# Expert stage of a three-block kernel: token parts moved from GpSimd to VectorE, and a new pinned order of an expert's steps

## The chip, the cores and the metric

The kernel runs on one core of one Trainium2 chip. The time is the device time of one execution in microseconds (us). 512 tokens pass through two dense blocks and then through a block that ends in a mixture of 32 experts.

## The reference, cut to what matters

The dense blocks (attention, convolution, a state-space mixer) are untouched by the change. What the change touches is the last part, for 512 tokens of 1024 features:

```python
combine = jnp.sum(jax.nn.one_hot(expert_id, N_EXPERTS, dtype=f32) * w[..., None], axis=1)
y = jnp.zeros_like(xt)
for e in range(N_EXPERTS):                      # 32
    h = jax.nn.silu(xt @ w_gate[e]) * (xt @ w_up[e])      # 1024 -> 256, twice
    y = y + combine[:, e:e + 1] * (h @ w_down[e])         # 256 -> 1024
```

Each token has two experts; their weights and places follow from a router that runs just before.

## The kernel before, in words

**Tiling.** The router sorts the 1024 pairs of token and expert by expert (`route`, L1536). The rows of the tokens are fetched in sorted order by indirect DMAs, transposed on TensorE, and kept in one tile `XT`, with features down the partitions and sorted places along the columns. Expert i takes 96 columns of `XT` from a place that is known only at run time (128 for one further job, number 32, that takes the overflow of a large expert). A loop over still more overflow closes the stage; its bound is read at run time.

**Two-part values.** A float32 product is made of three TensorE passes. Each operand is split into a high part (rounded to fp32r) and a low part (the value less its high part), and `mm3` (L298 to L300) multiplies high by high, high by low and low by high. So every weight tile needs a copy on ScalarE (`mh`, step h, L1716) and a subtraction on VectorE (`ml`, step l, L1722); each expert has six such pairs of 128x1024, numbered 0 to 5: 0 to 3 are gate and up weights, 4 and 5 are down weights. The expert's token columns need the same (`xh` and `xl`, step x, `tokens`, L1762).

**The steps of an expert** (`Expert.step`, L1710). x: token parts. h, l: weight parts. g0 to g3: six passes each of 128x512 into a PSUM tile `acc`. s: SiLU on ScalarE (L1734). m: product on VectorE (L1736), and the row numbers `ix` (L1738). t: two transposes on TensorE (L1742). a, b: parts of the transposed tile (ScalarE L1745, VectorE L1747). d0, d1: six passes each into a PSUM tile `s`. y0, y1: copies of the two halves into a tile `ye` on ScalarE (L1757); after y1 GpSimd issues an indirect DMA (L1759) that adds the 96 rows of `ye` to the output in DRAM.

**Order.** `moe` (L1432) walks over the 33 jobs. In one round, x is the round's expert, `prev` the one before, and `nxt` the one after. The string `MOE` (L67) is the order in which the steps are traced: h, l, g and the small x belong to the round's expert, H, L and X to the next one, the other letters to the one before. From round 2 on (`CHAIN`), `in_order` (L1489) makes every engine and the queues of SyncE and GpSimd take their instructions exactly in the traced order; before that the scheduler decides.

**Buffers and queues.** The raw weights come in three DMAs of 1 MB per expert, issued by SyncE, into a ring of nine tiles, so the next load into a tile waits for both subtractions that read it. `mh` has seven tiles, `ml` six, `ye` three, `xh` and `xl` two. The adds of rows into the output all write the same DRAM tensor, and each waits until the one before has landed. The first nine raw tiles are loaded during the block before.

**GpSimd's work before.** From expert 2 on (`POOL = 2`) `tokens` reads the place into a GpSimd register (L1769), makes `xh` with a copy (L1775) and `xl` with a subtraction (L1776), both on GpSimd. For experts 0 and 1 ScalarE and VectorE do it (L1771, L1772). The first four subtractions of expert 0 (`LPOOL = 4`) also run on GpSimd, ahead of the router; all other subtractions of experts 0 and 1 are held until the router's sort is done (`issue_after`).

Of the kernel before, what the change touches and what calls it, by code (L numbers as in the profile page):

```python
# [9 lines left out]
F32 = mybir.dt.float32  # L10
# [4 lines left out]
AF = mybir.ActivationFunctionType  # L15
OP = mybir.AluOpType
AX = mybir.AxisListType
PSUM = bass.MemoryType.PSUM
# [41 lines left out]
NRAW = (6, 2, 0, 1)  # L60
POOL = 2
LPOOL = 4
AHEAD = 2
CHAIN = 2
EXTRA = 29
ORDERED = (mybir.EngineType.PE, mybir.EngineType.Activation, mybir.EngineType.DVE, mybir.EngineType.Pool, mybir.EngineType.SP)
MOE = "X s m h2 g0 t a l2 b h3 g1 h4 d0 y0 l3 l4 h5 l5 d1 y1 H0 L0 g2 H1 L1 g3"  # L67
RW1 = (0, 0, 0, 0, 0, 0, 0, 0)
# [166 lines left out]
def prior(offset):  # L235
    """A method whose instructions the scheduler takes earlier, by so many places."""
    def deco(f):
        def g(self, *a, **k):
            with self.tc.high_priority(offset=offset):
                return f(self, *a, **k)  # L240
        return g
    return deco


class K:
# [36 lines left out]

# [1 line left out]
    def psum(self, pool, tag, shape=(128, 512)):  # L284
# [105 lines left out]
    def positions(self, pf):  # L390
        """Positions as float32, along the row and (negated) down the partitions."""
        nc, A = self.nc, self.A
        pi = self.T(self.xp, [128, 512], F32, "sq").bitcast(I32)
        nc.gpsimd.dma_start(pi, A["pos"].to_broadcast([128, 512]))
        nc.vector.tensor_copy(pf, pi)
        qi = self.T(self.smp, [128, 8], I32, "nyi")[:, :4]
        nc.gpsimd.dma_start(qi, A["pos"].rearrange("a (t p) -> p (a t)", p=128))
        posq = self.T(self.smp, [128, 4], F32, "posq")
        nc.vector.tensor_copy(posq, qi)
        nc.vector.tensor_scalar(posq, posq, -1.0, None, op0=OP.mult)  # L400
        return posq
# [14 lines left out]
    def distances(self, pf, posq):  # L416
        """Position biases of all heads, to DRAM."""
        nc = self.nc
        dist = self.T(self.ap, [128, QW], F32, "E")
        for t in range(4):  # L420
            n = 128 * (t + 1)
            nc.scalar.activation(dist[:, QOFF[t]:QOFF[t] + n], pf[:, :n], AF.Abs, bias=posq[:, t:t + 1])
        for h in range(6):
            B = self.T(self.ap, [128, QW], F32, "E")
            nc.vector.tensor_scalar(B, dist, -(2.0 ** (-8.0 * (h + 1) / 6)) * 32.0 ** 0.5, None, op0=OP.mult)
            nc.gpsimd.dma_start(self.Bd[h], B)
# [11 lines left out]

# [1 line left out]
    def x_in(self):  # L440
# [39 lines left out]

# [1 line left out]
    @prior(200)  # L482
    def pv(self, E, vt, hd, u):
        """E: probabilities up to a factor per query [128, QW]; writes the head's rows (head hd of a pair) of u."""
        nc = self.nc
# [28 lines left out]
    def vtile(self, src, part=None):  # L514
        """src: a pair's feature-major values, or a tile per head with its rows in part; gives token-major two-part tiles."""
        nc = self.nc
        vt = self.T(self.ap, [128, 2, 4, 2, 64], F32R, "V")
        bank = self.psum(self.pt, "t")
        bv = bank.rearrange("p (k b c) -> p k b c", k=4, b=2)
        ident = self.c("ident")  # L520
        for k in range(4):
            c = slice(128 * k, 128 * k + 128)
            if part is None:
                nc.tensor.transpose(bank[:, c], src[:, c], ident)
            else:
                for b in range(2):
                    nc.tensor.transpose(bv[:, k, b, :], src[b][part, c], ident[part, part])
        d = vt.rearrange("p b k a c -> p k b a c")
        self.split(d[:, :, :, 0, :], d[:, :, :, 1, :], bv)
        return vt  # L530

    @prior(200)
    def softmax(self, score, sm, bias=None, scale=1.0, mask=None):
        """Rows of one score map: exp(logit - max) in a [128, QW] tile, their sums per query tile in sm [128, 4]."""
        nc = self.nc
# [25 lines left out]
    def bcast2(self, f):  # L561
        """f: a factor per token and head of a pair [128, 4, 2]; gives it for the pair's feature rows (PSUM)."""
        pt = self.psum(self.pt, "t")
# [11 lines left out]
    def square_sums(self, u, r=None):  # L575
        """Per token and head of a pair: the sum of squares of u, times r twice."""
        nc = self.nc
# [9 lines left out]

# [1 line left out]
    def layer(self, l):  # L589
# [13 lines left out]
    def attention(self, l):  # L603
# [47 lines left out]
        def spill(i):  # L651
            """M-tile i of the projection, as exact two-part values, to DRAM."""
            acc = mtile(i)
# [25 lines left out]
        def norm_out(us, rs, sq, name):  # L679
            """Norm over all pairs; sq: their square sums per token and head."""  # L680
            v = sq[0]
# [270 lines left out]

# [1 line left out]
    def mixer(self):  # L954
# [28 lines left out]
        def gate(i, spare, d=None):  # L983
            """sigmoid of gate tile i; kept on chip, or in DRAM."""
            acc = mtile(i, spare)
# [111 lines left out]
    def moe_in(self):  # L1097
        """What the experts need that does not depend on their tokens."""
        nc, A, M = self.nc, self.A, self.rt
# [29 lines left out]
    def x_out(self, x, m, gain, racc):  # L1129
        """A finished tile of the residual stream: to the output and, times the gain, to the rows the experts read."""  # L1130
        nc = self.nc
# [20 lines left out]
    def sin_cos(self, pool, ang, k, lo, shape, sin_scale):  # L1152
        """ang: exact multiples (reduced in place by k turns), lo: what is added after; gives (cos, sin * sin_scale)."""
        nc = self.nc
# [213 lines left out]
    def forget_spill(self, mtile, R, p, j):  # L1368
        """Queries (j = 0) or keys (1) of a pair, normalised, as two-part values, or its values (2): to DRAM."""
        nc, sp = self.nc, self.sp  # L1370
# [55 lines left out]

# [1 line left out]
    def mc(self, name):  # L1428
# [3 lines left out]
    def moe(self):  # L1432
        nc, tc, A = self.nc, self.tc, self.A
        with ExitStack() as c:
# [31 lines left out]
            x = start(0)  # L1466
            x.run("x h0 l0 h1 l1")
            for n in range(len(seq)):
# [3 lines left out]
                for what in MOE.split():  # L1472
                    k, j = what[0], int(what[1:] or 0)
                    if k in "hlgx":
                        y = x
# [6 lines left out]
                prev, x = x, nxt  # L1482
            prev.run("s m t a b d0 y0 d1 y1")
            self.in_order(mark)
# [4 lines left out]
    def in_order(self, mark):  # L1489
        """Each engine takes what was traced since mark in the order in which it was traced."""  # L1490
        last = {}
# [6 lines left out]
    def dynamic(self, i):  # L1498
        """The i-th of the jobs on the list: its weights, records, what drops its empty rows, and its place."""
        nc = self.nc  # L1500
# [9 lines left out]
    def records(self, off, n):  # L1510
        """Token, weight and norm factor of n sorted places from off."""
        nc = self.nc
# [8 lines left out]
    def first_max(self, x, m, n, iota):  # L1521
        """One-hot of the first maximum along the last axis of x [128, m, n], and the maximum."""
        nc, P = self.nc, self.rt
# [172 lines left out]
class Expert:  # L1696
    """One run of rows through one expert's weights, in steps."""

    def __init__(self, K, i, we, sl, big, off, n=128):
        """off: where the first of the n columns of XT stands, on chip (None: at 0)."""  # L1700
        self.K, self.i, self.sl, self.big, self.off, self.n = K, i, sl, big, off, n
# [8 lines left out]
    def step(self, k, j):  # L1710
# [6 lines left out]
        elif k == "l":  # L1717
            hi, lo, w = self.W[j]
            pool = (self.i, j) < (0, LPOOL)
            after = K.tc.issue_after(K.routed) if self.i < 2 and not pool else ExitStack()  # L1720
            with after:
                (nc.gpsimd if pool else nc.vector).tensor_tensor(lo, w, hi.bitcast(F32), op=OP.subtract)  # L1722
        elif k == "x":
# [38 lines left out]
    def tokens(self):  # L1762
        K, n, nc = self.K, self.n, self.K.nc
        self.x = x = tuple(K.T(K.mx, [128, KD, n], F32R, t) for t in ("xh", "xl"))

        def cols(eng):
            if self.off is None:
                return K.XT[:, :, 0:n]
            return K.XT[:, :, bass.ds(eng.value_load(self.off, min_val=0, max_val=2 * S), n)]  # L1769
        if self.i < POOL:  # L1770
            nc.scalar.activation(x[0], cols(nc.scalar), AF.Copy)  # L1771
            nc.vector.tensor_tensor(x[1], cols(nc.vector), x[0].bitcast(F32), op=OP.subtract)  # L1772
        else:
            src = cols(nc.gpsimd)
            nc.gpsimd.tensor_copy(x[0], src)  # L1775
            nc.gpsimd.tensor_tensor(x[1], src, x[0].bitcast(F32), op=OP.subtract)  # L1776

# [16 lines left out]
```

## Time and profile before

| what | value |
|---|---|
| median of 3 runs | 2154.57 us |
| lowest and highest run | 2150.1 and 2155.29 us |
| span of the profiled execution | 2153.1 us (its whole time was not recorded apart from the span) |
| TensorE busy | 94% of the span |
| VectorE busy | 71% |
| ScalarE busy | 51% |
| GpSimd busy | 10%, nearly all of it in the last sixth |

The span is divided by the page into 40 slices. In the last eight, the expert stage with the router ahead of it, VectorE is busy for nine tenths of most slices and the 16 DMA engines for eight or nine tenths, with 313 to 327 GB/s in the six slices of the steady part. TensorE is granted its full clock (2.4 GHz) in nearly all slices. Busy time counts an instruction from its start to its end, also where it was held up inside.

### The profile page before, as it was taken

The numbers are of one execution on the slowest core, as the hardware profiler recorded it, in microseconds if no ns is written. First come the engines' busy times: TensorE is split into PE (matmuls) and PEld (weight loads), VectorE is DVE, ScalarE is ACT, GpSimd is POOL, SyncE is SP. The second block draws the span as 40 slices with busy tenths as digits, with TensorE's granted clock in tenths as the row PEclk, the third lists the DMA queues.
The fourth block names the chain that finished last, engine by engine and source line by source line (L and its number), as shares of the span: only waits on it lengthen the run. The fifth ranks groups of instructions, "written<-read, shape, count | busy, mean of one in ns | idle before, by whom it ended". The sixth has DMA issues, their size and how long they took to land.

```text
span 2153.1 us, 28938 instructions
## 1 busy us (share of the span) xinstructions
PE 2026.8 (94%) x10024; PEld 1586.3 (74%) x10024; DVE 1520.0 (71%) x2705; ACT 1087.3 (51%) x1765; POOL 218.4 (10%) x222
## 2 busy tenths in 40 slices
PE   6999999999999999899999999999999967888896
PEld 5776778888888777678888888788878745555554
DVE  5678787777534588787777535887565676999996
ACT  4475544444323376554444323433574445777774
POOL 2000000000000000000000000000000024445553
PEclk9999999999999999999999999999999978999998
DMA  4455542222344445542222343434463837998992
GB/s 151 145 163 185 193 159 91 97 98 98 108 131 134 144 127 175 177 159 88 98 98 98 105 132 118 153 124 123 148 179 136 278 97 238 313 315 314 319 327 70
DMA packets 133461, 344.88 MB, mean 160 GB/s; under 512 B 28634, under 2 KB 41946, under 8 KB 120642
## 3 DMA queue, kind: packets, MB, share of 16 engines
q1 hardware_dynamic: 127394, 330.29, 46.7%
q0 software_dynamic: 5920, 12.74, 2.3%
q8 instruction: 80, 1.31, 0.2%
q14 instruction: 67, 0.55, 0.1%
HBM read 294.27 MB, written 51.15 MB: 160 GB/s over the span
## 4 chain that ended last, share of the span: by engine, by line
PE 77%; DVE 10%; issue 5%; DMA 4%; ACT 3%; POOL 0%; SPq 0%; DVEq 0%; POOLq 0%; ACTq 0%
PE acc L298 19%; PE acc L300 19%; PE acc L299 19%; DVE ml L1722 2%; PE t L495 2%; PE t L339 2%; PE s L300 2%; PE t L566 1%; DMA raw<-in_we 1%; PE s L298 1%; PE s L299 1%; DVE ix L1738 1%; PE o L508 1%; PE o L507 1%; DMA ye<-xrd,idx 1%
## 5 line engine op out<-in xcount | busy, mean ns | idle before, releaser
L298 PE MATMUL acc<-hb,wh 128*128 128x512 f32 x1400 | 558.5, 399 | 19.1 <-ACT hb L293 13.9
L299 PE MATMUL acc<-hb,wh 128*128 128x512 f32 x1400 | 557.3, 398 | 2.8 <-DVE hb L294 2.0
L300 PE MATMUL acc<-hb,wl 128*128 128x512 f32 x1400 | 556.9, 398 | 1.0 <-DVE wl L291 1.0
L290 ACT ACTIVATE wh<-w 128x1024 fp32r<-128x1024 f32 (+3 forms) x265 | 260.0, 981 | 522.5 <-PE acc L299 393.4
L291 DVE TENSOR_TENSOR wl<-w,wh 128x1024 fp32r<-128x1024 f32 (+3 forms) x265 | 299.7, 1131 | 151.2 <-ACT wh L290 149.1
L298 PEld LDWEIGHTS acc<-hb,wh 128*128 128x128 f32 x1400 | 266.8, 191 | 75.2 <-ACT hb L293 13.9
L299 PEld LDWEIGHTS acc<-hb,wh 128*128 128x128 f32 x1400 | 266.4, 190 | 56.8 <-DVE hb L294 3.8
L300 PEld LDWEIGHTS acc<-hb,wl 128*128 128x128 f32 x1400 | 266.4, 190 | 53.2 <-DVE wl L291 1.8
L1722 DVE TENSOR_TENSOR ml<-raw,mh 128x1024 fp32r<-128x1024 f32 x194 | 259.5, 1367 | 33.1 <-ACT mh L1716 23.9
L1716 ACT ACTIVATE mh<-raw 128x1024 fp32r<-128x1024 f32 x198 | 201.7, 1053 | 0.6 <-PE o L300 0.5
L300 PE MATMUL acc<-hid,wl 128*128 128x512 f32 x320 | 126.4, 395 | 0.0
L298 PE MATMUL acc<-hid,wh 128*128 128x512 f32 x320 | 126.4, 395 | 0.0
L299 PE MATMUL acc<-hid,wh 128*128 128x512 f32 x320 | 126.3, 395 | 0.0
L299 PE MATMUL acc<-ml,xh 128*96 128x512 f32 (+1 forms) x264 | 107.6, 408 | 4.9 <-DVE ml L1722 4.8
L895 POOL MEMSET raw<- 128x2 f32 x88 | 8.5, 100 | 999.8 <-DVE hb L291 512.8
L298 PE MATMUL acc<-mh,xh 128*96 128x512 f32 (+1 forms) x264 | 106.8, 404 | 0.2 <-ACT xh L1771 0.2
L300 PE MATMUL acc<-mh,xl 128*96 128x512 f32 (+1 forms) x264 | 105.4, 399 | 0.0
L896 DVE TENSOR_TENSOR raw<-acc,R 128x512 f32<-128x512 f32 x88 | 60.6, 688 | 60.7 <-PE acc L300 60.3
L550 ACT ACTIVATE E<-E,mx 128x128 f32<-128x128 f32 (+3 forms) x160 | 88.8, 555 | 28.9 <-DVE mx L548 28.3
L291 DVE TENSOR_TENSOR PT<-t,PT 128x512 fp32r<-128x512 f32 (+1 forms) x120 | 69.5, 596 | 20.1 <-ACT PT L290 19.4
L900 ACT ACTIVATE cv<-raw,sp 128x512 f32<-128x512 f32 x88 | 71.8, 816 | 18.1 <-DVE raw L896 18.1
L1776 POOL TENSOR_TENSOR xl<-XT,xh 128x768 fp32r<-128x768 f32 (+1 forms) x31 | 80.4, 2593 | 2.5
(462 smaller groups left out, 3507.8 us busy)
## 6 DMA issues: line engine op xcount, KB each, us to landing
raw<-in_we SPq DMA_DIRECT2D x99, 1024.0 KB, 7.4
w<-in_wfi SPq DMA_DIRECT2D x88, 512.0 KB, 3.3
w<-in_wp SPq DMA_DIRECT2D x38, 512.0 KB, 3.7
w<-in_wz SPq DMA_DIRECT2D x33, 512.0 KB, 3.7
w<-in_wfo SPq DMA_DIRECT2D x32, 512.0 KB, 3.5
hld<-tf SPq DMA_DIRECT2D x56, 256.0 KB, 2.7
qk<-hld SPq DMA_DIRECT2D x96, 128.0 KB, 3.4
qk<-hld SPq DMA_DIRECT2D x192, 64.0 KB, 1.9
```

The lines of the kernel that those rows point to most:

```text
L290: nc.scalar.activation(hi, src, AF.Copy)
L291: nc.vector.tensor_tensor(lo, src, hi.bitcast(F32), op=OP.subtract)
L298: mm(out, lh[0], rh[0], start=start, stop=False)
L299: mm(out, lh[0], rh[1], start=False, stop=False)
L300: self.last_mm = mm(out, lh[1], rh[0], start=False, stop=stop).ins
L339: self.nc.tensor.matmul(pt[:, n * t:n * t + n], sq[:, 128 * t:128 * t + 128], rhs, start=i == 0, stop=i == len(sqs) - 1)
L550: nc.scalar.activation(e, e, AF.Exp, bias=mx, scale=-1.0, accum_out=sm[:, qt:qt + 1])
L896: nc.vector.tensor_tensor(raw[:, 2:], acc, R, op=OP.mult)
L900: nc.scalar.activation(t, raw[:, 2:], AF.Identity, bias=sp[:, cb:cb + 1], scale=sp[:, cw + 2:cw + 3])
L1716: nc.scalar.activation(hi, w, AF.Copy)
L1722: (nc.gpsimd if pool else nc.vector).tensor_tensor(lo, w, hi.bitcast(F32), op=OP.subtract)
L1776: nc.gpsimd.tensor_tensor(x[1], src, x[0].bitcast(F32), op=OP.subtract)
```

## The change

It drops the two constants that gave GpSimd arithmetic, makes VectorE do both token parts of every expert, writes a new order of steps, and lets the next expert's third weight pair (H2, L2) and the previous expert's down weights (P4, Q4, P5, Q5) lie in the round. Comments and doc strings are removed as well. Apart from those, the diff is:

```diff
-POOL = 2
-LPOOL = 4
-MOE = "X s m h2 g0 t a l2 b h3 g1 h4 d0 y0 l3 l4 h5 l5 d1 y1 H0 L0 g2 H1 L1 g3"
+MOE = "s P4 m Q4 g0 P5 h3 Q5 g1 t a b H0 l3 g2 L0 H1 d0 y0 L1 X d1 H2 y1 L2 g3"
...
-            x.run("x h0 l0 h1 l1")
+            x.run("x h0 l0 h1 l1 h2 l2")
...
-                    if k in "hlgx":
+                    if k in "PQ":
+                        y, k = prev, "hl"["PQ".index(k)]
+                    elif k in "hlgx":
...
-            prev.run("s m t a b d0 y0 d1 y1")
+            prev.run("s h4 m l4 h5 t a b l5 d0 y0 d1 y1")
...
-            pool = (self.i, j) < (0, LPOOL)
-            after = K.tc.issue_after(K.routed) if self.i < 2 and not pool else ExitStack()
-            with after:
-                (nc.gpsimd if pool else nc.vector).tensor_tensor(lo, w, hi.bitcast(F32), op=OP.subtract)
+            with K.tc.issue_after(K.routed) if self.i < 2 else ExitStack():
+                nc.vector.tensor_tensor(lo, w, hi.bitcast(F32), op=OP.subtract)
...
-        if self.i < POOL:
-            nc.scalar.activation(x[0], cols(nc.scalar), AF.Copy)
-            nc.vector.tensor_tensor(x[1], cols(nc.vector), x[0].bitcast(F32), op=OP.subtract)
-        else:
-            src = cols(nc.gpsimd)
-            nc.gpsimd.tensor_copy(x[0], src)
-            nc.gpsimd.tensor_tensor(x[1], src, x[0].bitcast(F32), op=OP.subtract)
+        src = K.XT[:, :, 0:n] if self.off is None else K.XT[:, :, bass.ds(nc.vector.value_load(self.off, min_val=0, max_val=2 * S), n)]
+        nc.vector.tensor_copy(x[0], src)
+        nc.vector.tensor_tensor(x[1], src, x[0].bitcast(F32), op=OP.subtract)
```

GpSimd keeps the indirect DMAs. The number of weight parts, matmul passes, loads and row additions is the same.

## Rows read from the trace of the kernel before

**Rows 1.** The page: its first line.
```profile
span 2153.1 us, 28938 instructions
```
**Rows 2.** Windows: length, busy PE, PEld, DVE, ACT, POOL, then clock, DMA share, GB/s.
```profile
1820.00:2060.00 240.00, 212.30 (x885) 132.95 (x884) 222.29 (x212) 175.58 (x233) 119.67 (x69) 1.00 0.90 314
2061.00:2106.00 45.00, 41.36 (x176) 26.99 (x175) 43.39 (x43) 34.75 (x47) 23.87 (x13) 1.00 0.98 340
```
**Rows 3.** Groups by line and form, 1820 to 2080 us.
```profile
L1722 DVE TENSOR_TENSOR ml<-raw,mh 128x1024 fp32r<-128x1024 f32 x153 | 199.9, 1333 | 19.2 <-ACT mh L1716 19.2
L1776 POOL TENSOR_TENSOR xl<-XT,xh 128x768 fp32r<-128x768 f32 x25 | 64.7, 2587 | 2.0
```
**Rows 4.** Timeline of VectorE inside one steady round (start, length).
```profile
1938.99 3.04 DVE L1722 TENSOR_TENSOR ml<-raw,mh 128x1024 fp32r<-128x1024 f32 x2 [0.20 <-ACT mh L1716]
...
1942.34 1.39 DVE L1738 TENSOR_TENSOR ix<-sl,big 96x1 int32<-96x1 f32 x1
```
**Rows 5.** Timeline of GpSimd in the same round.
```profile
1941.02 2.70 POOL L1776 TENSOR_TENSOR xl<-XT,xh 128x768 fp32r<-128x768 f32 x1
```
**Rows 6.** Timeline of VectorE where GpSimd made no token part.
```profile
2094.57 0.47 DVE L1736 SCALAR_TENSOR_TENSOR a<-a,sl,acc 96x256 f32<-96x256 f32 x1
2094.96 0.14 DVE L1738 TENSOR_TENSOR ix<-sl,big 96x1 int32<-96x1 f32 x1
2095.03 1.21 DVE L1722 TENSOR_TENSOR ml<-raw,mh 128x1024 fp32r<-128x1024 f32 x1
2096.16 0.34 DVE L1747 TENSOR_TENSOR al<-t,ah 128x192 fp32r<-128x192 f32 x1
```
**Rows 7.** Timeline of VectorE: token part of expert 1, made there before.
```profile
1806.61 0.95 DVE L1772 TENSOR_TENSOR xl<-XT,xh 128x768 fp32r<-128x768 f32 x1
1807.48 0.15 DVE L1738 TENSOR_TENSOR ix<-sl,big 96x1 int32<-96x1 f32 x1
```
**Rows 8.** Groups of VectorE over the span: a float32 copy, SBUF to SBUF.
```profile
L1313 DVE COPY r<-mag 128x512 f32<-128x512 f32 x4 | 1.7, 419 | 0.0
```
**Rows 9.** Timeline of TensorE: first pass of d0, experts 0 and 1.
```profile
1811.25 0.47 PE L298 MATMUL s<-mh,ah 128*96 128x512 f32 x1
...
1819.87 0.40 PE L298 MATMUL s<-mh,ah 128*96 128x512 f32 x1
```
**Rows 10.** Timeline of GpSimd: the 1st, 28th, 29th and 33rd row addition.
```profile
1815.48 1.50 POOL L1759 DMA_INDIRECT out<-ye,ix  x1 [2.10 <-ACT ye L1757]
...
2094.28 1.68 POOL L1759 DMA_INDIRECT out<-ye,ix  x1 [4.12 <-ACT mh L1716]
...
2105.05 2.10 POOL L1759 DMA_INDIRECT out<-ye,ix  x1 [5.30 <-DVE ix L1738]
...
2142.06 1.43 POOL L1759 DMA_INDIRECT out<-ye,ix  x1 [5.82 <-ACTq L1486]
```
**Rows 11.** DMA issues, 1815 to 2060 us: count, median us to landing.
```profile
out<-ye,ix POOLq DMA_INDIRECT x24, 8.7
```
**Rows 12.** DMA issues, 2061 to 2098 us.
```profile
out<-ye,ix POOLq DMA_INDIRECT x4, 10.1
```
**Rows 13.** DMA issues, 2090 to 2099 us: the 28th row addition alone.
```profile
out<-ye,ix POOLq DMA_INDIRECT x1, 10.0
```
**Rows 14.** DMA issues, 2120 to 2153 us, after the last weights.
```profile
out<-ye,ix POOLq DMA_INDIRECT x3, 5.3
```
**Rows 15.** Timeline of VectorE near the end of the loads.
```profile
2106.53 11.51 DVE L1722 TENSOR_TENSOR ml<-raw,mh 128x1024 fp32r<-128x1024 f32 x5 [0.36 <-ACT mh L1716]
```
**Rows 16.** Timeline of GpSimd ahead of the router's sort.
```profile
1754.29 6.99 POOL L1722 TENSOR_TENSOR ml<-raw,mh 128x1024 fp32r<-128x1024 f32 x3 [253.97 <-ACT mh L1716]
```
**Rows 17.** Timeline of VectorE while expert 0 starts (idle before in brackets).
```profile
1792.37 1.23 DVE L1722 TENSOR_TENSOR ml<-raw,mh 128x1024 fp32r<-128x1024 f32 x1 [2.41 <-PE acc L299]
1798.49 0.18 DVE L1680 CAST lists<-lf 1x48 int32<-1x48 f32 x1 [4.90 <-DMA lf<-ld]
1805.47 1.23 DVE L1722 TENSOR_TENSOR ml<-raw,mh 128x1024 fp32r<-128x1024 f32 x1 [6.80 <-PE acc L299]
```
**Rows 18.** Line L1769: reading the place into a register, on VectorE's queue.
```profile
L1769 DVEq TENSOR_LOAD <-offs x1: 550/550/550, 1782.5 to 1782.5; - x1
```

More of the change, by code (lines that the diff above doesn't have):

```diff
@@ L1764, in tokens @@
         self.x = x = tuple(K.T(K.mx, [128, KD, n], F32R, t) for t in ("xh", "xl"))
[L1766 to L1769, printed above, removed]
-        if self.i < POOL:
-            nc.scalar.activation(x[0], cols(nc.scalar), AF.Copy)
-            nc.vector.tensor_tensor(x[1], cols(nc.vector), x[0].bitcast(F32), op=OP.subtract)
-        else:
-            src = cols(nc.gpsimd)
-            nc.gpsimd.tensor_copy(x[0], src)
-            nc.gpsimd.tensor_tensor(x[1], src, x[0].bitcast(F32), op=OP.subtract)
+        src = K.XT[:, :, 0:n] if self.off is None else K.XT[:, :, bass.ds(nc.vector.value_load(self.off, min_val=0, max_val=2 * S), n)]
+        nc.vector.tensor_copy(x[0], src)
+        nc.vector.tensor_tensor(x[1], src, x[0].bitcast(F32), op=OP.subtract)
 def kernel(**inputs):
```

## The prediction

> **What bounds the kernel now.** I read the page first for the span, 2153.1 us [rows 1], and its slices, which place the change in the last sixth. There the windows view tells how full each resource is: in the steady 240 us VectorE is busy for 0.93 of the time, the DMA engines for 0.90, TensorE for 0.88 [rows 2]. Three resources close to full mean that a gain for one is soon stopped by another, so each needs a price per expert. The period is read from the row additions: the first starts at 1815.48 and the 28th at 2094.28 [rows 10], 27 intervals in 278.8 us, **10.33 us** each.
>
> Next, why VectorE is full. A weight subtraction takes 1333 ns on average [rows 3]; where GpSimd makes no token part, one starts at 2095.03 and the next instruction at 2096.16, 1.13 us later [rows 6]. In a steady round two of them take 3.04 us and the tiny `ix` 1.39 us, while GpSimd's `xl` runs from 1941.02 to 1943.72 [rows 4, 5]; `ix` alone is 0.14 us [rows 6]. Per round that is 0.78 + 1.25 = 2.0 us in which VectorE is held, not working. The Trainium skill agrees (SBUF — State Buffer, "Who interferes with whom"): a VectorE instruction with two SBUF inputs and a GpSimd one that reads SBUF exclude each other.
>
> Last, the indirect DMAs, which busy times don't show. The 28th addition starts at 2094.28, lands 10.0 us later [rows 13], and the 29th starts at 2105.05 [rows 10]: 0.77 us after the landing, though its data were ready long before. So the additions form **a chain of their own**, one landing plus 0.77 us each. With the DMA engines at 0.90 a landing takes 8.7 us [rows 11], which makes 9.47, still under 10.33; at 0.98 [rows 2] it takes 10.1 [rows 12], which makes 10.87.
>
> **The change part by part.** All per expert unless said.
> - *VectorE without GpSimd's arithmetic.* Six subtractions at 1.13 are 6.78; step m and `ix` 0.46 (2094.57 to 2095.03), `al` 0.34 at most [rows 6]. Added: `xl`, 0.87 from start to start [rows 7], and the copy `xh`, which no row shows at this size. The nearest is a copy of 512 in 419 ns [rows 8]; at the same rate per element 768 take 0.63, and never more than `xl` with two inputs, 0.95; I take 0.6, near the copy's own rate; the low end, half the time of two inputs, is 0.4. Sum 9.05; with the highest copy 9.4. Now it fills the 10.33.
> - *Reading the place on VectorE's queue.* 0.55 us on the one occasion [rows 18]. The subtraction L1 in front of it covers it, if the queue reads on while the engine works; from 0 to 0.55, I take 0, and the worst sum is then 9.95, still below 10.33.
> - *The new order.* I walked each engine through one round of 9.05 us, m at 0. VectorE: Q4, Q5, b by 3.1, l3, L0, L1 by 6.5, X by 8.0, L2 last. ScalarE's H2 follows y0 (about 4.8) and is done by 5.9, so L2 doesn't wait; s, P4, P5 lie before the next Q4, Q5. TensorE gets `xl` at 8.0 and needs 8.62 per round (1811.25 to 1819.87, [rows 9]), so it stays just behind. Weight tiles: `ml` is rewritten six parts later, after its last pass. Cost 0 beside VectorE's sum; cover gone, TensorE's 8.62 is next.
> - *SyncE's queue.* Raw tile 2 of an expert is now freed by Q5, a round later than by l5, and the next expert's first load queues behind it. Nine tiles are three experts; the load is needed about two rounds after issue, against a landing of some 8 us. Cost 0.
> - *DMA floor.* 0.90 of 10.33 is 9.3 us of moving per expert [rows 2]: the engines can't go below that, so 9.3, not 9.05, is the pace of the rest.
> - *The chain of additions.* At a pace of 9.3 the DMA engines never rest, and the chain needs 10.87. It then falls behind by 1.57 us per expert until the three `ye` tiles are used up: an addition may be late by three paces less a landing and the 2 us from y0 to its start, 27.9 - 10.1 - 2 = 15.8 us. That is ten experts. From there the chain sets the pace. Between (0.90; 8.7) and (0.98; 10.1) a landing grows by 17.5 us per unit of share; the pace P with P = landing + 0.77 and share 9.3/P is 10.0 (share 0.93, landing 9.2). So the first 93 us pass 8.6 additions at 10.87, the other 18.4 of the 27 intervals take 10.0: 93.5 + 184 = 277.5, against 278.8: **-1.3**.
> - *The last five experts.* From the 28th to the 33rd addition it takes 47.8 us now [rows 10]. Five subtractions are stretched to 11.51 us there while GpSimd works beside them [rows 15]; that goes. The weights are all in, a landing takes 5.3 [rows 14], the chain 6.07 each. The engines need four rounds of 9.05 and a last, short one of about 6, 42 us, of which 15.8 are already done by their lead, leaving 26. So the chain ends last: five at 6.07, 30.4, against 47.8: **-17.4**. The final h4, l4, h5, l5, now behind s (about 1.5 us more than before), are covered by the 4 us between 26 and 30; without that lead they are paid.
> - *The start.* GpSimd's subtractions for expert 0 (three in 6.99, the fourth alone [rows 16]) go to VectorE, 4.5 us after the sort. VectorE idles 2.41 + 4.90 + 6.80 us there [rows 17], but the first must be done before g0: from 0 to 4.5, I take 1.0. In round 1 d0 now follows g2, six passes later than before, 1.4: **+2.4**.
>
> Sum: -1.3 - 17.4 + 2.4 = **-16** against the span of 2153.1. The median of the runs is 2154.57, 1.5 above the span for what lies around it, and I subtract from the median: **2138.6 us**.
>
> **The rivals.**
> - *Landings stay at 8.7* although the loads run closer together. For it: at a share of 0.90 single landings are well under the period. Then the chain needs 9.47: 27 intervals 255.7 (-23), lateness only 27 x 0.17 = 4.6, and the tail 42 - 4.6 = 37.4 (-10.4). With +2.4: -31, 2123.6.
> - *The DMA queue never rests.* The new order frees three raw tiles within about 1.5 us of a round, so loads come in a burst and every landing may take 10.1. 27 x 10.87 = 293.5 (+14.7), tail -17.4, start +2.4: -0.3, 2154.3, **no change**.
> - *Slower: the copy holds up the addition.* Same landings, and VectorE's `xh` falls on the moment when GpSimd prepares the rows. The row: the addition at 2105.05 takes 2.10 us on GpSimd beside a working VectorE, the last one 1.43 beside an idle one [rows 10]. Held for a whole copy, 0.6, the chain is 11.47: 27 intervals 309.7 (+30.9), five at 6.67 33.4 (-14.4), start +2.4: +19, 2173.6. It decides only where the chain has taken over; below a landing of about 9.8 it can't turn the sign. Against it: X and the addition lie 2 us or more apart in my walk, and the copy is 0.6 of 9 us. The Trainium skill speaks for it (SBUF — State Buffer, "SBUF: two separate sides"): a float32 copy from SBUF to SBUF on VectorE locks GpSimd out, and it can't write descriptors meanwhile. By that rule the result would be this rival's; whether a copy does so in this kernel no row of before shows.
> - *The change doesn't do what it says:* the stretch has another cause than GpSimd's arithmetic. VectorE, busy 0.93 of 10.33 or 9.6 [rows 2], would then need 1.5 more for the token parts, 11.1: 27 x 0.75 = +20; with the last five as now and the start's 2.4, 2177. Against it: `ix` falls from 1.39 to 0.14 exactly where GpSimd pauses.
>
> **How the numbers follow.** The forecast and what lies close to it (landings of 9 to 9.6) gets 0.42, landings unchanged 0.27, the queue that never rests 0.19, the held addition 0.08, the stretch of other cause 0.04. 0.3% is 6.5 us, about what a measurement of this kernel can tell from no change. Faster: the first two, 0.69, with a little of the third, 0.70. Same: most of the third, 0.17. Slower: the last two and the rest, 0.13. The range leaves out the two slow cases and the outermost of the fast one: 2124 to 2158.
>
> **What would show it.** In the profile after, GpSimd shows only indirect DMAs; subtractions stand at 1.13 to 1.2 us, `ix` at 0.14, `xh` near 0.6. The DMA share of the steady part rises from 0.90 to 0.93 or more, and landings of the additions to 9 or more. ScalarE's y0 begins to wait for additions after ten experts or so, where VectorE then idles: the sign that the chain has taken over. The five last intervals shrink to 30 to 37 us. I am wrong if VectorE still has no gaps at a period near 10.3, if landings pass 10.4, if TensorE or the loads (waits of ScalarE's `mh` for raw tiles) hold a round, or if additions start without waiting for the one before.

## The result, and the profile after

The changed kernel takes **2130.2 us** (median of 4 runs, 2118.74 to 2131.5); the kernel before, run beside it on the same chip, takes 2154.93 us (4 runs, 2150.1 to 2156.46). The ratio is 0.9891 with a 95% interval of 0.987 to 0.9912: about 1.1% faster. (One of the 5 runs of the changed kernel's repeat, further down, took 2842.48 us at a mean granted clock of 0.65, against 0.97 to 0.98 in all other runs, and is left out of that repeat's figures.) The forecast was 2138.6, in a range of 2124 to 2158. The span of the profiled execution fell by 25.5 us, to:

```profile
span 2127.6 us, 28818 instructions
```

Cutting the span at the same events in both traces tells where that came from. The events are the first instruction of the router's norm on VectorE (`nv`), the router's sort (`srt`), and the starts of the 1st, 28th and 33rd row addition on GpSimd.

| stretch | before | after | difference |
|---|---|---|---|
| start to norm (untouched by the change) | 1751.69 | 1748.40 | -3.3 |
| norm to sort | 19.2 | 13.0 | **-6.2** |
| sort to 1st addition | 44.6 | 42.9 | -1.7 |
| 1st to 28th addition (27 intervals) | 278.8 | 277.9 | -0.9 |
| 28th to 33rd addition | 47.8 | 34.3 | **-13.5** |
| 33rd addition to end | 11.0 | 11.1 | +0.1 |

The first row is scatter: over the traces of this study, in which that stretch is the same code, `nv` starts between 1742.95 and 1755.16. So some 22 us are the change's, in two places, and only one of them was forecast.

The windows view of the steady stretch (columns as in [rows 2], to which it answers) and, below it, the median landing of the additions there (DMA issues, answering to [rows 11]):

```profile
1820.00:2060.00 240.00, 228.25 (x949) 141.29 (x948) 226.25 (x277) 184.41 (x249) 48.84 (x23) 1.00 0.92 338
```
```profile
out<-ye,ix POOLq DMA_INDIRECT x23, 9.1
```

GpSimd falls from 119.67 to 48.84 us, now additions alone. VectorE is *busier* than before, 226.25, with 277 instructions for 212: it does more, and is held less. The DMA engines move 338 GB/s for 314, at a share of 0.92 for 0.90. VectorE's groups from 1820 to 2040 us, by shape (answering to [rows 3, 8]):

```profile
L1720 DVE TENSOR_TENSOR ml<-raw,mh 128x1024 fp32r<-128x1024 f32 x138 | 162.6, 1218 | 11.5 <-ACT mh L1716 10.0
...
L1765 DVE CAST xh<-XT 128x768 fp32r x23 | 12.7, 551 | 0.0
```

The timeline of VectorE shows one whole early round and, further on, VectorE's first wait for ScalarE in this stretch:

```profile
1841.77 0.47 DVE L1734 SCALAR_TENSOR_TENSOR a<-a,sl,acc 96x256 f32<-96x256 f32 x1
1842.16 0.15 DVE L1736 TENSOR_TENSOR ix<-sl,big 96x1 int32<-96x1 f32 x1
1842.23 2.35 DVE L1720 TENSOR_TENSOR ml<-raw,mh 128x1024 fp32r<-128x1024 f32 x2
1844.50 0.34 DVE L1745 TENSOR_TENSOR al<-t,ah 128x192 fp32r<-128x192 f32 x1
1844.77 3.48 DVE L1720 TENSOR_TENSOR ml<-raw,mh 128x1024 fp32r<-128x1024 f32 x3
1848.17 0.55 DVE L1765 CAST xh<-XT 128x768 fp32r x1
1848.75 0.96 DVE L1766 TENSOR_TENSOR xl<-XT,xh 128x768 fp32r<-128x768 f32 x1
...
1851.22 2.35 DVE L1720 TENSOR_TENSOR ml<-raw,mh 128x1024 fp32r<-128x1024 f32 x2
...
1895.66 1.22 DVE L1720 TENSOR_TENSOR ml<-raw,mh 128x1024 fp32r<-128x1024 f32 x1 [0.92 <-ACT mh L1716]
```

From 1842.23 to 1851.22 a round takes 8.99 us, without a stretch and without a wait. At 1895.66, some ten experts in, VectorE starts to wait for ScalarE, and the waits view (us in total, times, longest; 1820 to 2060 us) says what ScalarE itself waits for, the landings of the additions that free `ye`:

```profile
ACT ye L1755 <- DMA out<-ye,ix: 41.3, 16, 3.4
```

GpSimd's timeline shows that chain (the 1st, 5th, 6th, 8th, 28th, 30th and 33rd addition, answering to [rows 10]):

```profile
1804.28 1.48 POOL L1757 DMA_INDIRECT out<-ye,ix  x1 [24.29 <-ACT ye L1755]
...
1842.18 7.83 POOL L1757 DMA_INDIRECT out<-ye,ix  x1 [8.04 <-DVE ml L1720]
1858.62 1.42 POOL L1757 DMA_INDIRECT out<-ye,ix  x1 [8.61 <-ACT a L1732]
...
1878.20 7.84 POOL L1757 DMA_INDIRECT out<-ye,ix  x1 [8.03 <-DVE ml L1720]
...
2082.20 1.42 POOL L1757 DMA_INDIRECT out<-ye,ix  x1 [7.84 <-DVE xh L1765]
...
2095.41 3.68 POOL L1757 DMA_INDIRECT out<-ye,ix  x1 [4.37 <-DVE ml L1720]
...
2116.47 1.42 POOL L1757 DMA_INDIRECT out<-ye,ix  x1 [4.44 <-DMA out<-ye,ix]
```

Most take GpSimd 1.4 to 2.5 us. Three are long: 7.83, 7.84 and 3.68. Since each addition waits for the landing of the one before, such an excess goes whole into the chain: from 1842.18 to 1858.62 are 16.4 us where 9.5 to 10 is usual.

The landings of the nine additions from 1800 to 1895 us, the ten experts for which the prediction took 10.1 us:

```profile
out<-ye,ix POOLq DMA_INDIRECT x9, 9.1
```

The last view is of the router, whose own code the diff leaves as it is. VectorE's timeline there, before:

```profile
1751.69 0.16 DVE L347 TENSOR_SCALAR nv<-t 128x4 f32<-128x4 f32 x1 [0.55 <-PE t L339]
...
1754.60 2.06 DVE L1584 COPY val<-ny 128x8 f32<-128x8 f32 x1
...
1759.01 2.31 DVE L1552 TENSOR_TENSOR eg<-L,gm 128x16 f32<-128x16 f32 x1
...
1770.87 0.40 DVE L1614 TENSOR_REDUCE srt<-rtmp 128x8 f32<-128x256 f32 x1
```

and after:

```profile
1748.40 0.16 DVE L345 TENSOR_SCALAR nv<-t 128x4 f32<-128x4 f32 x1 [1.35 <-PE t L337]
...
1751.76 0.16 DVE L1584 COPY val<-ny 128x8 f32<-128x8 f32 x1
...
1752.40 0.17 DVE L1552 TENSOR_TENSOR eg<-L,gm 128x16 f32<-128x16 f32 x1
...
1761.40 0.40 DVE L1614 TENSOR_REDUCE srt<-rtmp 128x8 f32<-128x256 f32 x1
```

A copy of eight elements per partition took 2.06 us before and takes 0.16 now, and `eg` goes from 2.31 to 0.17. GpSimd's early subtractions of expert 0 ran from 1754.29 [rows 16], right beside them.

### The profile page after: what moved, and what is told of

The parts are those of the page before. It is cut to its first block, busy times and chain, and to the rows that moved or that the text cites. A ratio compares the mean times of both kernels' runs of the same rounds, so it can differ in the third digit from the quotient of the medians.

```text
span 2127.6 us, 28818 instructions
## 1 busy us (share of the span) xinstructions
PE 2025.4 (95%) x10024; PEld 1583.7 (74%) x10024; DVE 1501.3 (71%) x2774; ACT 1080.5 (51%) x1763; POOL 110.3 (5%) x155
## 4 chain that ended last, share of the span: by engine, by line
PE 74%; DVE 10%; DMA 8%; ACT 4%; issue 3%; POOL 0%; SPq 0%; DVEq 0%; POOLq 0%; ACTq 0%
PE acc L296 19%; PE acc L298 19%; PE acc L297 19%; DVE ml L1720 4%; DMA out<-ye,ix 3%; PE t L493 2%; PE t L337 2%; DMA raw<-in_we 2%; PE t L564 1%; ACT mh L1716 1%; PE o L506 1%; DMA sl<-stab 1%; PE o L505 1%; DMA ye<-xrd,idx 1%; PE o L297 1%
## 5 line engine op out<-in xcount | busy, mean ns | idle before, releaser
L1720 DVE TENSOR_TENSOR ml<-raw,mh 128x1024 fp32r<-128x1024 f32 x198 | 233.5, 1218 | 20.3 <-ACT mh L1716 12.7
L1757 POOL DMA_INDIRECT out<-ye,ix x33 | 68.1, 2063 | 269.8 <-ACT ye L1755 122.7
L493 PE MATMUL t<-cst,E 128*128 128x128 f32 x400 | 71.7, 283 | 4.6 <-DVE E L811 2.7
```

What stands on the lines that cost most here:

```text
L493: nc.tensor.transpose(bank[:, c:c + 128], E[:, QOFF[qt] + 128 * kt:QOFF[qt] + 128 * kt + 128], self.c("ident"))
L1720: nc.vector.tensor_tensor(lo, w, hi.bitcast(F32), op=OP.subtract)
L1757: nc.gpsimd.indirect_dma_start(out=K.out, out_offset=bass.IndirectOffsetOnAxis(ap=self.ix, axis=0), in_=self.y, in_offset=None, bounds_che ...
```

## The experiments

Each ratio is to the kernel before on the same chip, with its 95% interval. "Router" is the time from `nv` to `srt`, "loaded" that from the 1st to the 28th addition, "tail" that from the 28th to the 33rd: 19.2, 278.8 and 47.8 us before; 13.0, 277.9 and 34.3 after.

**Where the start was won.** The first edit takes, from the kernel before, only GpSimd's four early subtractions; the second gives them back to the changed kernel.

```diff
-LPOOL = 4
+LPOOL = 0
```


> The kernel before with one edit: the first four subtractions of expert 0 run on VectorE after the sort, not on GpSimd ahead of it. Theory (the start): GpSimd's four subtractions hold four of the router's VectorE instructions for about 2 us each, 8 us in all, and the rest of the stage follows that. Then the first row addition starts near 1807 us instead of 1815.5 and the time is 8 lower, 2147. Rival (my predicted step, +1 for moving the work to VectorE): the first addition stays at 1815 to 1817 and the time at 2155 to 2156; the earlier start in the changed kernel then comes from its order.

```diff
-            with K.tc.issue_after(K.routed) if self.i < 2 else ExitStack():
-                nc.vector.tensor_tensor(lo, w, hi.bitcast(F32), op=OP.subtract)
+            pool = (self.i, j) < (0, 4)
+            with K.tc.issue_after(K.routed) if self.i < 2 and not pool else ExitStack():
+                (nc.gpsimd if pool else nc.vector).tensor_tensor(lo, w, hi.bitcast(F32), op=OP.subtract)
```


> The changed kernel with that one part undone: the first four subtractions back on GpSimd. Theory (the start): the first row addition moves from 1804 back to 1812 to 1815, time 2138 to 2141. Rival (the order does it): 1804 and 2130, unchanged.

The first gave 2139.21 us, ratio 0.9932 [0.9911, 0.9953], router 13.0; the second 2134.66, ratio 0.9915 [0.9893, 0.9938], router 19.3. VectorE's timeline in the router, of the first:

```profile
1751.07 0.16 DVE L347 TENSOR_SCALAR nv<-t 128x4 f32<-128x4 f32 x1 [1.36 <-PE t L339]
...
1764.07 0.40 DVE L1614 TENSOR_REDUCE srt<-rtmp 128x8 f32<-128x256 f32 x1
```

and of the second:

```profile
1751.78 0.16 DVE L345 TENSOR_SCALAR nv<-t 128x4 f32<-128x4 f32 x1 [0.54 <-PE t L337]
...
1771.06 0.40 DVE L1614 TENSOR_REDUCE srt<-rtmp 128x8 f32<-128x256 f32 x1
```

The 6.2 us go and come with those four subtractions, in either kernel. That settles where the 6.2 us come from. The first additions stand at 1807.56 and 1812.48 us, as expected. The times are not: the first is some 8 us lower than expected, the second 3 us below its range. The kernel before takes 2150.97 us on that chip, which accounts for 4 us of either; in the first kernel "loaded" is also 3.2 us shorter than before (275.6), for a reason that was not followed. The four subtractions also cost VectorE next to nothing after the sort: from there to the first addition it takes 43.5 us in the first kernel against 44.6 before.

**Arithmetic or order?** Three kernels separate the two halves of the steady change. The first keeps the new order but gives the token parts from expert 2 on back to GpSimd; the second keeps the old order, and its early subtractions on GpSimd, but makes all token parts on VectorE; the third is the second with X moved to the place that I took to be what mattered in the new order.

```diff
-        src = K.XT[:, :, 0:n] if self.off is None else K.XT[:, :, bass.ds(nc.vector.value_load(self.off, min_val=0, max_val=2 * S), n)]
-        nc.vector.tensor_copy(x[0], src)
-        nc.vector.tensor_tensor(x[1], src, x[0].bitcast(F32), op=OP.subtract)
+        eng = nc.vector if self.i < 2 else nc.gpsimd
+        src = K.XT[:, :, 0:n] if self.off is None else K.XT[:, :, bass.ds(eng.value_load(self.off, min_val=0, max_val=2 * S), n)]
+        eng.tensor_copy(x[0], src)
+        eng.tensor_tensor(x[1], src, x[0].bitcast(F32), op=OP.subtract)
```


> The changed kernel with the token parts of the experts from 2 on back on GpSimd, new order kept. Theory (GpSimd's arithmetic holds VectorE): VectorE's stretch comes back, subtractions near 1.33 us, a round of 10.0 to 10.5 us and a slow end, time 2142 to 2150; the start keeps its gain. Rival (the new order is what shortens the round and the end): 2130 to 2133, with subtractions that may be long but off the path.

2142.13 us, ratio 0.9955 [0.9936, 0.9975]; loaded 283.6, tail 50.1, in the trace of an execution of 2151.08 us, the slowest of five. VectorE's subtractions are stretched again (groups by shape, 1820 to 2040 us). Three additions take 8.6 to 8.8 us; GpSimd's timeline shows one of them, and VectorE's the four subtractions that end with it, with no token part among them:

```profile
L1720 DVE TENSOR_TENSOR ml<-raw,mh 128x1024 fp32r<-128x1024 f32 x127 | 172.7, 1409 | 1.3 <-ACT mh L1716 1.3
```
```profile
1930.53 8.81 POOL L1757 DMA_INDIRECT out<-ye,ix  x1 [4.53 <-DVE ml L1720]
...
1940.26 3.88 POOL L1767 TENSOR_TENSOR xl<-XT,xh 128x768 fp32r<-128x768 f32 x1
```
```profile
1933.42 4.61 DVE L1720 TENSOR_TENSOR ml<-raw,mh 128x1024 fp32r<-128x1024 f32 x4
```

The second, old order and all parts on VectorE:

```diff
-        if self.i < POOL:
...
-            nc.gpsimd.tensor_copy(x[0], src)
-            nc.gpsimd.tensor_tensor(x[1], src, x[0].bitcast(F32), op=OP.subtract)
+        src = K.XT[:, :, 0:n] if self.off is None else K.XT[:, :, bass.ds(nc.vector.value_load(self.off, min_val=0, max_val=2 * S), n)]
+        nc.vector.tensor_copy(x[0], src)
+        nc.vector.tensor_tensor(x[1], src, x[0].bitcast(F32), op=OP.subtract)
```


> The kernel before with the token parts of all experts on VectorE, old order and the four early subtractions on GpSimd kept. Theory (arithmetic, not order): start as before (first addition 1815), no stretch, the 27 loaded intervals 270 to 279 us, the last five 34 to 42 instead of 47.8: time 2138 to 2148. Rival (the order is needed): the old order's waits (ScalarE's weight parts, late g0) keep a round at 10.3 or above, time 2154 to 2165.

2161.85 us, ratio 1.0048 [1.0032, 1.0063]: **slower** than before, loaded 291.5. The stretch is gone (`ml` 1222 ns, `ix` 149 ns), yet a round takes 10.53 us (from the subtraction at 1944.16 to the same one at 1954.69), because VectorE waits for ScalarE's high parts. From 1820 to 2040 us it waits so 62 times, 29.7 us in total, up to 2.2 each. The rival (the order is needed) forecast this. The timeline:

```profile
1944.16 1.22 DVE L1722 TENSOR_TENSOR ml<-raw,mh 128x1024 fp32r<-128x1024 f32 x1
...
1948.99 1.23 DVE L1722 TENSOR_TENSOR ml<-raw,mh 128x1024 fp32r<-128x1024 f32 x1 [0.67 <-ACT mh L1716]
...
1954.69 1.21 DVE L1722 TENSOR_TENSOR ml<-raw,mh 128x1024 fp32r<-128x1024 f32 x1
```

The third:

```diff
-MOE = "X s m h2 g0 t a l2 b h3 g1 h4 d0 y0 l3 l4 h5 l5 d1 y1 H0 L0 g2 H1 L1 g3"
+MOE = "s m h2 g0 t a l2 b h3 g1 h4 d0 y0 l3 l4 h5 l5 d1 y1 H0 L0 X g2 H1 L1 g3"
```


> The old order with the token parts on VectorE, as in the run with the old order, but X moved from the head of the round to between L0 and g2; all else of the old order kept. Theory (in the old order X stood between L1 and m, on the loop from one expert's product through transposes, d, y and the next weight parts back to m, and 1.4 us on VectorE there went straight into the round of 10.5 us): the round falls to 9.1 to 9.7 us and the chain of additions takes over, loaded intervals near 270 to 278 us, last five 34 to 40, time 2136 to 2144. Rival (the old order needs the down weights' parts moved as well): the round stays above 10.2 us, time 2152 to 2162.

2152.66 us against 2152.65, ratio 1.0011 [0.9989, 1.0034], loaded 281.4. A round still takes 10.48 us on VectorE (1941.87 to 1952.35), and VectorE still waits for ScalarE's high parts (0.69 us before 1946.72):

```profile
1941.87 1.22 DVE L1722 TENSOR_TENSOR ml<-raw,mh 128x1024 fp32r<-128x1024 f32 x1
...
1946.72 1.23 DVE L1722 TENSOR_TENSOR ml<-raw,mh 128x1024 fp32r<-128x1024 f32 x1 [0.69 <-ACT mh L1716]
...
1952.35 1.21 DVE L1722 TENSOR_TENSOR ml<-raw,mh 128x1024 fp32r<-128x1024 f32 x1
```

So my theory, that the place of the token parts is what counts in the new order, fell. What is shown: VectorE's share alone buys no short round, nor does the order alone; both together do. (The first kernel's 0.4% is no more than its earlier start: the kernel before with that start alone has 0.7%.) Why the old order holds VectorE is argued, not shown, and no run moves the down weights' parts or H2 and L2 alone: in the old order m, t, a, h3, h4, y0, h5, y1, H0, H1 and the next m hang on each other within one round, through ScalarE again and again, while the new order takes P4, Q4, P5, Q5 from the expert before and H2, L2 for the one after, so that VectorE has a part at hand that waits for nothing of this round.

**Is the chain of additions the bound?** Three kernels. The first sends every other expert's additions of the changed kernel to a second DRAM tensor (their parts are then missing from the output), the second does the same to the kernel before, the third gives the changed kernel a fourth `ye` tile (and one `mh` tile less, for the room).

```diff
-                nc.gpsimd.indirect_dma_start(out=K.out, out_offset=...
+                nc.gpsimd.indirect_dma_start(out=K.out if self.i % 2 == 0 else K.out2, out_offset=...
```


> The changed kernel, but the row additions of the odd-numbered experts go to a scratch tensor in DRAM, so an addition waits only for the one two before it; the output lacks those experts' parts. Theory (the chain of additions sets the pace once VectorE is free): ScalarE's y0 no longer waits for additions, the 27 loaded intervals fall from 278 to about 9.3 each, 250 us, the last five are then the engines' own, about 42: time near 2110. Rival (the pace is set by VectorE, TensorE or the loads, and the waits of y0 only show slack): intervals stay at 10.0 to 10.3, time 2126 to 2132.

2112.59 us, ratio 0.983 [0.9807, 0.9852]; loaded 250.7, tail 45.2. GpSimd's timeline (1st, 7th, 8th, 28th and 33rd addition) and what ScalarE waits for in place of additions, 1820 to 2060 us:

```profile
1802.37 1.48 POOL L1759 DMA_INDIRECT out<-ye,ix  x1 [23.85 <-ACT ye L1757]
...
1855.69 1.44 POOL L1759 DMA_INDIRECT out<-ye,ix  x1 [7.56 <-ACT ye L1757]
1864.72 1.42 POOL L1759 DMA_INDIRECT out<-ye,ix  x1 [7.59 <-ACT ye L1757]
...
2053.06 1.42 POOL L1759 DMA_INDIRECT out<-ye,ix  x1 [5.91 <-ACT ye L1757]
...
2098.31 1.42 POOL L1759 DMA_INDIRECT out<-ye,ix  x1 [7.41 <-ACT ye L1757]
```
```profile
ACT mh L1718 <- DMA raw<-in_we: 24.4, 23, 1.9
```

Without the chain the 3rd to the 13th addition come every 9.0 us, VectorE's round; from there to the 28th it is 9.56 us, where ScalarE waits for loads. No addition of "loaded" takes more than 2.5 us here, so of the 27 us that "loaded" loses some 13 belong to the two long additions, which are links of the chain too. The additions follow the experts directly, so no lead is built up, and the tail is long again. The chain, long additions included, is the bound of the changed kernel, and the short tail is the same thing seen from its end.

> The kernel before with the additions of the odd-numbered experts to a scratch tensor; the output lacks their parts. Theory (the chain was covered before by the slower VectorE): the steady round stays at 10.3 and only the intervals near the end of the loads shorten; 1 to 5 us less than the kernel before. Rival (the chain already set the pace before): 15 us or more less.

2151.81 us, ratio 1.0008 [0.9997, 1.0019]; loaded 277.5. The 1 to 5 us that were expected don't show in the time. Before the change the chain was covered, as the prediction took it.

```diff
-"ye": 3 ... "mh": 7
+"ye": 4 ... "mh": 6
```


> The changed kernel with four tiles ye instead of three (and six tiles mh instead of seven, for room). Theory (the chain's own length counts, the ye tiles only set how far the rest may run ahead): y0's waits shrink, the end moves little, 2122 to 2131. Rival (the tiles are what binds): y0 no longer waits and the time falls by 10 or more, 2118 or less.

2130.86 us, ratio 0.9918 [0.9895, 0.994]; loaded 279.5; y0 waits 35.3 us, 14 times, for 41.3 and 16. One more buffer moves the wait and does not shorten it: a chain is not helped by a place to queue. (This trace has three long additions of 6.76 to 7.93 us where the changed kernel has two, so the comparison is not of the buffer alone.)

**What are the long additions?** The prediction's slower rival named VectorE's copy. The first edit below takes the copy away from VectorE; the second moves X forward by some 3.4 us in the round. Both start from the changed kernel, and the changed kernel and the first edit ran once more beside the second.

```diff
-        nc.vector.tensor_copy(x[0], src)
+        srca = K.XT[:, :, 0:n] if self.off is None else K.XT[:, :, bass.ds(nc.scalar.value_load(self.off, min_val=0, max_val=2 * S), n)]
+        nc.scalar.activation(x[0], srca, AF.Copy)
```


> The changed kernel with the high token part made by ScalarE instead of VectorE (the copy gone from VectorE). Theory 1 (the copy locks GpSimd out while it prepares an addition): no addition takes more than about 2.5 us on GpSimd, the two of 7.8 us are gone, 12 us less in the chain, 2114 to 2120. Theory 2 (it is the unbroken run of subtractions, and GpSimd gets in only at a gap of VectorE): additions that start just before Q4 still take 6 us or more where VectorE has no gap; 2124 to 2132.

2120.52 us, ratio 0.9863 [0.9841, 0.9884]; loaded 269.4. Neither theory's figures came out: the time lies between the two ranges, and one long addition is left in "loaded", of 5.73 us, beside a VectorE that makes no copy of token parts. GpSimd's timeline, and VectorE's:

```profile
1856.54 5.73 POOL L1757 DMA_INDIRECT out<-ye,ix  x1 [8.36 <-ACT mh L1716]
```
```profile
1855.48 3.48 DVE L1720 TENSOR_TENSOR ml<-raw,mh 128x1024 fp32r<-128x1024 f32 x3
1858.88 0.95 DVE L1767 TENSOR_TENSOR xl<-XT,xh 128x768 fp32r<-128x768 f32 x1
1859.76 1.22 DVE L1720 TENSOR_TENSOR ml<-raw,mh 128x1024 fp32r<-128x1024 f32 x1
1860.89 0.47 DVE L1734 SCALAR_TENSOR_TENSOR a<-a,sl,acc 96x256 f32<-96x256 f32 x1
```

It ends at 1862.27; less the 1.42 us of a free addition that is 1860.85, the end of the run of subtractions. In the changed kernel the one from 1842.18 ends at 1850.01, less 1.42 is 1848.59: the end of the copy, where the timeline shown above has the round's only gap (1848.72 to 1848.75). So I let the gap come earlier:

```diff
-MOE = "s P4 m Q4 g0 P5 h3 Q5 g1 t a b H0 l3 g2 L0 H1 d0 y0 L1 X d1 H2 y1 L2 g3"
+MOE = "s P4 m Q4 g0 P5 h3 Q5 g1 t a b X H0 l3 g2 L0 H1 d0 y0 L1 d1 H2 y1 L2 g3"
```


> The changed kernel with step X moved in the order from before d1 to right after b, so that VectorE's copy and the subtraction that needs it stand between Q5 and l3 instead of between L1 and L2; nothing else changes. Theory (an addition that GpSimd begins to prepare in VectorE's unbroken run waits for the run's first gap, and the gap is that between the copy and its dependent subtraction): the longest additions take 4 to 5 us on GpSimd instead of 7.8, because the gap now comes about 3 us after Q4 begins; time 3 to 6 us below the changed kernel. Rival (what holds it is the copy itself, or the delay has nothing to do with VectorE's order): additions of 7 to 8 us stay as often as before, time the same within 3 us.

2124.03 us, ratio 0.9872 [0.9853, 0.9891]; loaded 274.8. The long additions take 4.45, 3.94 and 4.44 us, as the theory had it; the gain in time over the changed kernel that ran beside it, 0.0007 of the ratio, is not clear of the noise. One of them on GpSimd, and VectorE beside it:

```profile
1840.98 4.45 POOL L1757 DMA_INDIRECT out<-ye,ix  x1 [8.00 <-DVE ml L1720]
```
```profile
1841.06 2.35 DVE L1720 TENSOR_TENSOR ml<-raw,mh 128x1024 fp32r<-128x1024 f32 x2
...
1843.59 0.55 DVE L1765 CAST xh<-XT 128x768 fp32r x1
1844.17 0.96 DVE L1766 TENSOR_TENSOR xl<-XT,xh 128x768 fp32r<-128x768 f32 x1
```

It ends at 1845.43, less 1.42 is 1844.01: again the end of the copy, wherever the copy stands. The two kernels that ran beside it:

> The changed kernel itself once more on this chip, as the reference for the other two; both theories 2119 to 2132, with a few additions above 5 us on GpSimd, not always at the same experts.

> The changed kernel with the high token part on ScalarE once more, beside the changed kernel. If the shorter VectorE round is what shortens the chain (more gaps, fewer long additions), it stays 5 to 10 us below the changed kernel; if the earlier difference was the chips', the two agree within 3 us.

The changed kernel again: 2127.8 us (median of four), 0.9879 [0.9859, 0.9898], with additions of 8.08 and 7.93 us. The copy on ScalarE again: 2121.93 us, 0.9852 [0.9834, 0.9871], loaded 270.4, one long addition of 5.50. On both chips it is the fastest of the kernels that give the whole output, ahead of the changed kernel by 0.0028 and 0.0027 of the ratio; the intervals overlap, so a gain of some 0.3% is likely and not settled.

Which additions are held depends on where in VectorE's round they start. Six traces of the new order have VectorE make the copy: the changed kernel, its repeat, four subtractions back on GpSimd, four `ye`, X earlier, two targets. Among the first 28 additions of each, eleven are long (3.94 to 8.16 us), and all eleven start 0.09 to 1.48 us after a step m does; none of the others, at most 2.47 us long, starts less than 4 us after one. The chain's step, some 9.9 us, is longer than VectorE's undisturbed round of 8.99, so the start drifts through the round: in the changed kernel it lies 0.43 us ahead of m at 1832.34, 0.41 after it at 1842.18, is held, and drifts to m again at 1878.20. Once VectorE waits for ScalarE, the round follows the chain and the additions start some 2 us ahead of m, and none is held again. With the copy on ScalarE this does not hold: four that start 1.08 to 1.29 us after m take less than 2 us, and the two long ones start some 4 us after m.

## Why the prediction was right, and where a step failed

- **What bounds the kernel: half of it.** GpSimd's arithmetic held VectorE, as read: the hold comes back with it (token parts on GpSimd again: 1409 ns a subtraction). But with the hold gone and the old order kept a round takes 10.53 us, so the old order, by VectorE's waits for ScalarE, held the round near 10.5 as well, and the prediction did not name it as a bound.
- **VectorE's sum: right.** 9.05 us forecast, 8.99 in the trace; `xh` 0.55 for the 0.6 taken, `ix` 0.15. No gap shows for reading the place on VectorE's queue.
- **The new order at no cost: right in the number,** and understated: I priced it as cover that is not lost. The kernel with the old order shows that without it the round stays at 10.5 and the change loses 0.5%.
- **DMA floor: right in size, wrong in what would show it.** With the chain cut in two the loads hold a round at some 9.56 us (9.3 forecast), though only from the 13th addition on; until then the round is VectorE's 9.0, below what I had called a floor. And "the DMA share rises to 0.93 or more" failed: 0.92, while GB/s rose by 8%.
- **The chain of additions takes over: right.** Landings 9.1 us for the 9.2 forecast, and the kernel with two targets loses the wait. That the first wait came after ten experts or so, as worked out, is in part luck: 12.8 of the 15.8 us of lead went into the two long additions. Without them a chain of 9.87 us against a round of 8.99 would have needed some 18 experts (an estimate from these figures); with X earlier, where the holds cost 5.5 us, the first y0 to wait is the 15th, not the 11th. The rival with landings of 8.7 and the one with 10.1 both fall with that row.
- **27 intervals, 277.5 forecast, 277.9 measured: right by two errors.** The two additions of 7.83 and 7.84 us cost about 6.4 each over 1.42, together 12.8; without them it would be 265, or 9.8 an interval, where the working gave 10.3 on average. (The copy on ScalarE, with one hold of 5.73, has 269.4, and less its 4.3 again 265; the same subtraction gives 262 to 269 in the other whole kernels of the new order with VectorE's token parts.) The term that was too large is the landing of 10.1 for the first ten experts: it was 9.1 there too. So the unhindered chain is faster than I had it, and **the step that I left to the slower rival happened**, only otherwise sized: not 0.6 us on every addition, but 6.4 on two of them. Of that rival's story the place was right (GpSimd prepares the rows while VectorE works) and the copy wrong: with the copy on ScalarE two holds remain (5.73, and 5.50 in its repeat), and with both token parts on GpSimd additions take up to 8.82. The Trainium skill (SBUF — State Buffer, "SBUF: two separate sides") says that a float32 copy on VectorE locks GpSimd out of writing descriptors; beside the copy itself the trace shows little: the addition at 2072.56 starts 0.05 us into one and takes 1.79 us, 0.37 over a free one. The remark of the same page's "Who interferes with whom" that a two-input operation does not stall descriptors, given there as inferred, does not account for these runs, and the measurement decides. Whether GpSimd was kept from writing descriptors or from reading the row numbers in SBUF, no run separates.
- **The last five, 30.4 forecast, 34.3 measured.** The mechanism held (a lead of the experts over the chain, then short landings); the held addition of 3.68 and landings that come down to 5.3 only by and by make the 3.9 us.
- **The start: the step that failed.** I took +2.4 from the sort on, for work that moves to VectorE; measured from the norm to the first addition it is 63.8 before and 55.9 after, -7.9. The step "GpSimd's subtractions for expert 0 go to VectorE" counted only what VectorE gains in work after the sort, and looked on [rows 16] as a cost to be moved. I had priced the stretch by GpSimd in the steady round and not asked the same of the router's rows beside those subtractions. Two runs show it: 13.0 us without the four, 19.3 with them. From the sort to the first addition it is -1.7 where I took +2.4, so the added work cost nothing there.

The sum: -16 forecast, -25.5 in the spans, of which -3.3 is scatter. The other 6 are errors that cancel in part: the start came out 10.3 us better than forecast, the last five 3.9 worse, and the 27 intervals right by the two errors above. So the forecast of 2138.6 owes its nearness to 2130.2 partly to luck. What stays open: which instructions of VectorE exactly keep GpSimd from preparing an addition, and why those that start at m are let in only at the copy. The lowest of the four runs, 2118.74, lies 11 us under the others, about what two long additions cost; no trace of that run shows whether it had any. Additions by experts of one parity write rows of the same tensor that are not all the same; dropping the wait between them in a kernel that keeps the whole output was not tried.

## What to carry to other kernels

When an engine's arithmetic is taken off a shared path, look along its whole timeline for short instructions that take 2 us beside it, not only in the loop the change is about. When a round gets shorter, ask which chain of transfers was covered by its old length, add landing and issue, and compare: here a chain of 9.9 us (a landing of 9.1 and 0.77) set the pace once the round fell from 10.3 to 9.0. And test an order and a placement apart, since each alone bought nothing here.

## What the runs showed of the hardware that was not expected

- GpSimd's preparation of an indirect DMA, 1.42 us when free, took up to 8.2 us beside an unbroken run of VectorE, mostly two-input float32 subtractions (8.8 in the kernel with the token parts on GpSimd, where VectorE runs no copy). Each of the six that I followed ends 1.42 us after that run does, to within 0.15 us: at the end of the copy with the short gap behind it (1848.59 and 1884.62; 1844.01 with X earlier; 1852.32 and 1879.31 in the repeated run), or at the first product that reads PSUM (1860.85, without the copy). The short subtraction `al` in between did not free them, though an addition of 3.27 us, in the kernel with the token parts on GpSimd, came free where `al` begins.
- An eight-element copy took 2.06 us for 0.16 beside a GpSimd subtraction of 128x1024.
- The DMA engines moved 314 GB/s at a share of 0.90, 338 at 0.92 and 350 at 0.95 (two targets): here the share was a poor measure of the room that was left.
